# Attention in a two-layer trunk: the first map's scaling on ScalarE, norm factors inside the weight splits, four buffers for turned maps

## The chip, the cores and the metric

The kernel runs on one core of a Trainium2 chip, as one launch. The core has TensorE (PE in the profile, with its weight loads apart as PEld), VectorE (DVE), ScalarE (ACT), GpSimd (POOL), and SyncE (SP), which issues most DMAs. The metric is the device time in microseconds.

## The reference, cut to what matters

The input is 1024 positions of 1024 float32 features. Layer 0 is a diagonal state-space layer with a gated output; the change does not touch it. Layer 1 is causal differential attention with 8 heads. Each head has two score maps of 64-wide queries and keys and one 128-wide value:

```
xn = rmsnorm(h, g)                      # g: one gain per feature, for K/V and for Q/z
qz = xn @ in_w;  kv = xn @ kv_w         # q, k get a partial rotary embedding
p  = softmax(q1 k1^T / 8) - lam * softmax(q2 k2^T / 8)      # causal
o  = rmsnorm(p @ v, subln_g) * (1 - lam_init) * silu(z)
h  = h + o @ out_w                      # and a final rmsnorm
```

## The kernel before

All matrices stay close to float32 accuracy by a split: a tile is written as a rounded half, hi, and the rest, lo = x - hi, and each product is three matmuls (hi hi, hi lo, lo hi; `mm3`, L159 to L161). So every weight tile that comes from HBM is first split.

`load_m` does that for a weight tile of 128x1024: a DMA into the one buffer mraw (L739), for normed inputs a multiplication by the gain on GpSimd (L741), the cast to hi on ScalarE (L742), the subtraction to lo on VectorE (L743). `load_early` does the same once, for the keys of head 0, into tiles of the pool `pp`. Of the loads with a gain, k, q and gate have eight slices of 128 output columns with one gain per partition in each slice; the value loads (L785) have four slices of 256 columns.

Layer 1 goes through 32 steps, 4 blocks of 256 queries for each of 8 heads. In a step the scores of the next step are emitted first, then the projections of the next head by a fixed plan (nothing, keys, queries, gate and, for every second head, values), then this step's maps are transposed (`turn`) and multiplied by the values (`mix`).

`scores` handles two query blocks of 128 rows. For each, TensorE writes both maps into PSUM (L833, L834), VectorE adds the mask and takes the row extreme (L839), ScalarE takes the exponential with the row sum beside it (L841), VectorE inverts both sums in one instruction (L844), makes rho = sum1 * lam / sum2 (L845) and e1 + rho * e2 (L847), and GpSimd scales the result by 1/sum1 (L848). L is the number of keys, 128 to 1024.

`turn` transposes a map in 128x128 blocks into PSUM (L866) and splits it into ph (ScalarE, L868) and pl (VectorE, L869), one pair of tiles for two key blocks, so up to four pairs in a step. The pool `pp` has three buffers of each. `mix` multiplies them by the values (L882 to L884); `head_norm` (L899 to L907) follows with the norm and the gate.

In `project_kq` a copy of a projection, xe, is taken to SBUF (L759), and four DMAs move its rotary rows into another tile (L763), which GpSimd multiplies (L764). In `gate` a tile e holds the clamped gate (L699), which goes three times through ScalarE (L700 to L702) before VectorE uses it (L703). Both tiles have the name ze and share two buffers.

The order of instructions on each engine is not the order of the code: the framework plans it, from its own estimates of what each instruction takes, and places waits on semaphores. Each engine then works through its list in order.

Of the kernel before, what the change touches and what calls it, by code (L numbers as in the profile page):

```python
# [18 lines left out]
P = 128  # L19
# [35 lines left out]
class Trunk:  # L55
# [635 lines left out]
    def gate(self, h, zg):  # L691

        nc = self.nc
        V, G, S = nc.vector, nc.gpsimd, nc.scalar
        for hs, pt in self.project(self.I["b_in_w"], D + h * P, self.sm("gb")):
            z = self.tq.tile([P, 512], F32, name="z", tag="xr", bufs=3)
            e = self.tq.tile([P, 512], F32, name="ze", bufs=2)
            V.tensor_mul(z, pt, self.R1[:, hs])  # L698
            V.tensor_scalar(e, z, -80.0, None, op0=ALU.max)  # L699
            S.activation(e, e, AF.Exp, scale=-1.0)  # L700
            S.activation(e, e, AF.Ln, bias=1.0)
            S.activation(e, e, AF.Exp, scale=-1.0)  # L702
            V.scalar_tensor_tensor(z, z, self.small1[:, 0:1], e, op0=ALU.mult, op1=ALU.mult)  # L703
            nc.sync.dma_start(zg[:, hs], z)
# [14 lines left out]
    def load_early(self, src, col, gain):  # L719

        nc = self.nc
        raw = self.wp.tile([P, KT, P], F32, name="mraw", bufs=self.wraw)
        nc.sync.dma_start(raw, src[:, col:col + P].rearrange("(k p) n -> p k n", p=P))
        nc.gpsimd.tensor_mul(raw, raw, gain.unsqueeze(2).broadcast_to([P, KT, P]))
        w = []
        for k in range(0, KT, 4):
            hi, lo = (self.pp.tile([P, 4, P], F32R, name=n) for n in ("ph", "pl"))
            nc.scalar.copy(hi, raw[:, k:k + 4])
            nc.vector.tensor_sub(lo, raw[:, k:k + 4], rd(hi))
            w += [(hi[:, j, :], lo[:, j, :]) for j in range(4)]  # L730
        return w

    def load_m(self, src, k0, nk, col, n, gain=None, slots=None):

        nc = self.nc
        pool, names = slots or (self.wp, ("mhi", "mlo"))
        hi, lo = (pool.tile([P, nk, n], F32R, name=x) for x in names)
        raw = self.wp.tile([P, nk, n], F32, name="mraw", bufs=self.wraw)
        nc.sync.dma_start(raw, src[k0 * P:(k0 + nk) * P, col:col + n].rearrange("(k p) n -> p k n", p=P))  # L739
        if gain is not None:  # L740
            nc.gpsimd.tensor_mul(raw, raw, gain[:, k0:k0 + nk].unsqueeze(2).broadcast_to([P, nk, n]))  # L741
        nc.scalar.copy(hi, raw)  # L742
        nc.vector.tensor_sub(lo, raw, rd(hi))  # L743
        return hi, lo

    def project_kq(self, h, src, gain, kind, w=None):
# [7 lines left out]
            out = [self.st.tile([P, SEQ], F32R, name=f"k{i}") for i in range(2)]  # L754
        for i, (hs, pt) in enumerate(self.project(src, h * P, gain, early=h == 0 and kind == "q", w=w)):
            xr = self.tq.tile([P, 512], F32, name="xr", bufs=3)
            xe = self.tq.tile([P, 512], F32, name="ze", bufs=2)
            xs = self.xs[i]
            S.copy(xe, pt)  # L759
            V.tensor_mul(xr, pt, self.RC[:, hs])  # L760
# [53 lines left out]
    def scores(self, ks, qs, qb):  # L814
# [5 lines left out]
        for i in (2 * qb, 2 * qb + 1):  # L820
# [14 lines left out]
            for m in range(2):  # L835
# [5 lines left out]
                S.activation(em[:, :L], em[:, :L], AF.Exp, bias=nmx[:, m:m + 1], scale=-1.0,  # L841
                             accum_out=sm[:, m:m + 1])
                e.append(em)
            V.reciprocal(rr, sm)  # L844
            V.scalar_tensor_tensor(rho, sm[:, 0:1], self.small1[:, 1:2], rr[:, 1:2], op0=ALU.mult, op1=ALU.mult)  # L845
            p = e[0]
            V.scalar_tensor_tensor(p[:, :L], e[1][:, :L], rho, p[:, :L], op0=ALU.mult, op1=ALU.add)  # L847
            G.tensor_scalar(p[:, :L], p[:, :L], rr[:, 0:1], 1.0, op0=ALU.mult, op1=ALU.mult)  # L848
            out.append(p)
        return out  # L850

# [62 lines left out]
    def layer1(self, dbg=None):  # L914
# [5 lines left out]
        with ExitStack() as es:  # L920
# [17 lines left out]
            for z in self.padded:  # L938
                for x in z:
                    G.memset(x.bitcast(F32), 0.0)  # L940
            self.ep, self.pp, self.op, self.tiny = pool("ep", 2), pool("pp", 3), pool("op", 2), pool("tiny", 4)
            self.pst, self.pss = pool("pst", 2, space=PSUM), pool("pss", 2, space=PSUM)
            self.psm = self.rp.enter_context(tc.tile_pool(name="psm", bufs=2, space=PSUM, side="right",
                                                          reuse_waits="tile"))
# [226 lines left out]
```

## Time and profile before

| what | us |
|---|---|
| median of 3 runs | 1117.68 (1115.88 to 1118.76) |
| profiled execution, its own time | 1121.34 |
| its span | 1119.6 |
| PE busy | 1070.6 |
| DVE busy | 820.1 |
| ACT busy | 546.3 |
| POOL busy | 361.9 |

The span runs from the first to the last instruction. Matmuls overlap and their ends are modelled, so that a busy PE is not always PE at its peak; the idle time of its weight loads shows more.

### The profile page before, as it was taken

The page shows a single profiled execution, that of the slowest core. Times are in us where ns is not written, and L with a number is a line of the kernel's source. Part 1 is how long each engine was busy: PE and PEld are TensorE (multiplying, and loading weights), DVE is VectorE, ACT ScalarE, POOL GpSimd, SP SyncE. Part 2 cuts the span into 40 slices and gives each one's busy share as a digit, 9 for nine tenths or more (in the row PEclk, how much of TensorE's full clock was granted, in tenths as well). Part 3 has the DMA queues.
Part 4 walks back from the last instruction along what each step waited for, and adds up shares of the span by engine and source line. Part 5 has one row for each costly group of instructions (what it writes and reads, how often), then busy time and mean ns, then how long its engine had stood idle before and what let it go on. Part 6 is the DMA issues. An engine that isn't in the chain of part 4 may idle for free.

```text
span 1119.6 us, 17333 instructions
## 1 busy us (share of the span) xinstructions
PE 1070.6 (96%) x6308; PEld 907.6 (81%) x6308; DVE 820.1 (73%) x1362; ACT 546.3 (49%) x1141; POOL 361.9 (32%) x333
## 2 busy tenths in 40 slices
PE   7999999998999999999999999999999999999996
PEld 5688888886888888988877987889878798777796
DVE  7799999974576443557977659867597767885466
ACT  6432433234444332435755655656556466674463
POOL 0000000000564014324543345343453535421258
PEclk9999999998999999999999999999999999999998
DMA  9143555455644444123221222122221122552344
GB/s 283 37 144 124 172 171 154 141 171 199 215 132 132 150 132 169 57 57 97 65 62 44 70 65 73 52 62 72 62 75 57 57 76 79 152 167 81 94 139 158
DMA packets 143140, 125.92 MB, mean 112 GB/s; under 512 B 9808, under 2 KB 123216, under 8 KB 143056
## 3 DMA queue, kind: packets, MB, share of 16 engines
q1 hardware_dynamic: 134736, 120.63, 34.9%
q10 hardware_dynamic: 8320, 4.19, 1.2%
q8 instruction: 49, 0.80, 0.3%
q14 instruction: 35, 0.29, 0.1%
HBM read 85.48 MB, written 33.03 MB: 106 GB/s over the span
## 4 chain that ended last, share of the span: by engine, by line
PE 41%; DVE 29%; ACT 9%; DMA 9%; issue 6%; POOL 3%; SPq 2%; DVEq 0%; POOLq 0%; ACTq 0%
PE ps L159 6%; PE ps L160 6%; PE ps L161 6%; DVE w L310 5%; DMA xs<-ze 3%; DVE mlo L743 2%; PE pm L159 2%; PE pm L161 2%; ACT e L841 2%; PE pm L160 2%; PE pm L803 2%; PE pm L805 2%; PE pm L804 2%; SPq L763 2%; DVE e L839 2%
## 5 line engine op out<-in xcount | busy, mean ns | idle before, releaser
L743 DVE TENSOR_TENSOR mlo<-mraw,mhi 128x1024 fp32r<-128x1024 f32 (+1 forms) x75 | 97.8, 1304 | 61.0 <-ACT mhi L742 60.9
L159 PE MATMUL pm<-h1h,mhi 128*128 128x512 f32 x352 | 139.7, 397 | 1.7 <-DVE xr L760 1.6
L161 PE MATMUL pm<-h1h,mlo 128*128 128x512 f32 x352 | 139.6, 397 | 0.0
L160 PE MATMUL pm<-h1l,mhi 128*128 128x512 f32 x352 | 139.3, 396 | 0.0
L841 ACT ACTIVATE e<-e,tiny 128x256 f32<-128x256 f32 (+7 forms) x128 | 99.4, 777 | 80.6 <-DVE tiny L839 80.3
L742 ACT CAST mhi<-mraw 128x1024 fp32r<-128x1024 f32 (+1 forms) x75 | 77.8, 1037 | 118.4 <-PE ps L160 62.8
L839 DVE CUSTOM_DVE_ANT_0 e<-s,tri 128x256 f32<-128x256 f32 (+7 forms) x128 | 94.6, 750 | 17.1 <-PE s L834 5.9
L848 POOL TENSOR_SCALAR e<-e,tiny 128x128 f32<-128x128 f32 (+3 forms) x64 | 60.9, 952 | 119.4 <-DVE e L847 96.3
L159 PE MATMUL ps<-xh,mhi 128*128 128x512 f32 x208 | 82.2, 395 | 1.9 <-DVE evo L491 1.9
L161 PE MATMUL ps<-xh,mlo 128*128 128x512 f32 x208 | 81.9, 394 | 0.0
L160 PE MATMUL ps<-xl,mhi 128*128 128x512 f32 x208 | 81.7, 393 | 0.0
L159 PEld LDWEIGHTS pm<-h1h,mhi 128*128 128x128 f32 x352 | 66.5, 189 | 14.4 <-DVE xr L760 2.4
L161 PEld LDWEIGHTS pm<-h1h,mlo 128*128 128x128 f32 x352 | 66.6, 189 | 12.6
L160 PEld LDWEIGHTS pm<-h1l,mhi 128*128 128x128 f32 x352 | 66.5, 189 | 12.3
L833 PE MATMUL s<-k,q 128*128 128x384 f32 (+4 forms) x192 | 67.4, 354 | 7.3 <-DVE tiny L839 5.7
L803 PE MATMUL pm<-mhi,h1h 128*128 128x256 f32 x224 | 64.4, 289 | 1.7 <-DVE z L698 1.1
L834 PE MATMUL s<-k,z 128*128 128x384 f32 (+4 forms) x192 | 65.5, 345 | 0.0
L869 DVE TENSOR_TENSOR pl<-t,ph 128x512 fp32r<-128x512 f32 (+2 forms) x112 | 54.8, 494 | 14.5 <-ACT ph L868 14.1
L741 POOL TENSOR_TENSOR mraw<-mraw,small 128x1024 f32<-128x1024 f32 x23 | 45.8, 1993 | 58.1 <-DMA mraw<-in_b_in_w 35.9
L805 PE MATMUL pm<-mhi,h1l 128*128 128x256 f32 x224 | 64.1, 287 | 0.0
L804 PE MATMUL pm<-mlo,h1h 128*128 128x256 f32 x224 | 63.6, 285 | 0.2 <-DVE mlo L743 0.2
L764 POOL TENSOR_TENSOR xs<-xs,RS 128x512 f32<-128x512 f32 x32 | 44.2, 1383 | 60.5 <-DMA xs<-ze 60.3
(374 smaller groups left out, 3019.7 us busy)
## 6 DMA issues: line engine op xcount, KB each, us to landing
mraw<-in_kv_w SPq DMA_DIRECT2D x16, 512.0 KB
mraw<-in_b_in_w SPq DMA_DIRECT2D x16, 512.0 KB
mraw<-in_in_w SPq DMA_DIRECT2D x13, 512.0 KB
ud<-evo SPq DMA_DIRECT2D x16, 256.0 KB
ug<-ud SPq DMA_DIRECT2D x8, 512.0 KB
kd<-ks SPq DMA_DIRECT2D x8, 512.0 KB
toep<-kd SPq DMA_DIRECT2D x8, 512.0 KB
yd<-yb ACTq DMA_DIRECT2D x8, 512.0 KB
```

The lines of the kernel that those rows point to most:

```text
L159: mm(ps, wh, xh, start=first, stop=False)
L160: mm(ps, wh, xl, start=False, stop=False)
L161: mm(ps, wl, xh, start=False, stop=last)
L742: nc.scalar.copy(hi, raw)
L743: nc.vector.tensor_sub(lo, raw, rd(hi))
L803: mm(o, self.h1h[k][:, ts], wh, start=k == 0, stop=False)
L804: mm(o, self.h1h[k][:, ts], wl, start=False, stop=False)
L805: mm(o, self.h1l[k][:, ts], wh, start=False, stop=k == KT - 1)
L833: mm(sps[m][:, c, :w], q2[m][:, qt], ks[m][:, cs], start=True, stop=False)
L834: mm(sps[m][:, c, :w], q2[2 + m][:, qt], ks[m][:, cs], start=False, stop=True)
L839: V.tensor_tensor_reduce(out=blocks(em[:, :L]), in0=sp[:, 0:nb, :w], in1=blocks(self.tri[:, SEQ - L:]), scale=-1.0, scalar=3e38, op0=ALU.a ...
L841: S.activation(em[:, :L], em[:, :L], AF.Exp, bias=nmx[:, m:m + 1], scale=-1.0, accum_out=sm[:, m:m + 1])
```

## The change

In `scores` VectorE inverts each row sum by itself, right after its exponential; ScalarE multiplies the first map by its inverse sum in place, rho becomes lam / sum2, and the scaling on GpSimd is gone. In `load_early` and `load_m` the multiplication by the gain on GpSimd is gone; a new function `split` writes hi = raw * gain on ScalarE and lo = raw * gain - hi on VectorE, slice by slice, with the slice's gain per partition. The pool `pp` has four buffers of each tile in place of three; ze has one in place of two.

```
-            e = self.tq.tile([P, 512], F32, name="ze", bufs=2)
+            e = self.tq.tile([P, 512], F32, name="ze", bufs=1)
...
-        nc.gpsimd.tensor_mul(raw, raw, gain.unsqueeze(2).broadcast_to([P, KT, P]))
         w = []
         for k in range(0, KT, 4):
             hi, lo = (self.pp.tile([P, 4, P], F32R, name=n) for n in ("ph", "pl"))
-            nc.scalar.copy(hi, raw[:, k:k + 4])
-            nc.vector.tensor_sub(lo, raw[:, k:k + 4], rd(hi))
+            self.split(hi, lo, raw[:, k:k + 4], gain[:, k:k + 4])
             w += [(hi[:, j, :], lo[:, j, :]) for j in range(4)]
         return w
+    def split(self, hi, lo, raw, gain):
+        for k in range(raw.shape[1]):
+            g = gain[:, k:k + 1]
+            self.nc.scalar.activation(hi[:, k, :], raw[:, k, :], AF.Copy, scale=g)
+            self.nc.vector.scalar_tensor_tensor(lo[:, k, :], raw[:, k, :], g, rd(hi[:, k, :]), op0=ALU.mult,
+                                                op1=ALU.subtract)
...
         if gain is not None:
-            nc.gpsimd.tensor_mul(raw, raw, gain[:, k0:k0 + nk].unsqueeze(2).broadcast_to([P, nk, n]))
+            self.split(hi, lo, raw, gain[:, k0:k0 + nk])
+            return hi, lo
...
-            xe = self.tq.tile([P, 512], F32, name="ze", bufs=2)
+            xe = self.tq.tile([P, 512], F32, name="ze", bufs=1)
...
-            V.reciprocal(rr, sm)
-            V.scalar_tensor_tensor(rho, sm[:, 0:1], self.small1[:, 1:2], rr[:, 1:2], op0=ALU.mult, op1=ALU.mult)
+                V.reciprocal(rr[:, m:m + 1], sm[:, m:m + 1])
+                if m == 0:
+                    S.activation(em[:, :L], em[:, :L], AF.Copy, scale=rr[:, 0:1])
+            V.tensor_mul(rho, rr[:, 1:2], self.small1[:, 1:2])
             p = e[0]
             V.scalar_tensor_tensor(p[:, :L], e[1][:, :L], rho, p[:, :L], op0=ALU.mult, op1=ALU.add)
-            G.tensor_scalar(p[:, :L], p[:, :L], rr[:, 0:1], 1.0, op0=ALU.mult, op1=ALU.mult)
...
-            self.ep, self.pp, self.op, self.tiny = pool("ep", 2), pool("pp", 3), pool("op", 2), pool("tiny", 4)
+            self.ep, self.pp, self.op, self.tiny = pool("ep", 2), pool("pp", 4), pool("op", 2), pool("tiny", 4)
```

## Rows read from the trace of the kernel before

**Rows 1.** The page's head: the span.
```profile
span 1119.6 us, 17333 instructions
```

**Rows 2.** Stages: length, then busy us per engine (instructions), granted TensorE clock, DMA.
```profile
480.00:1065.00 585.00, 559.33 (x3160) 480.96 (x3159) 438.50 (x847) 339.24 (x771) 241.40 (x217) 1.00 0.27 77
640.00:660.00 20.00, 20.00 (x126) 18.16 (x126) 11.76 (x33) 10.86 (x30) 7.92 (x9) 1.00 0.23 65
680.00:700.00 20.00, 17.65 (x85) 14.10 (x86) 19.40 (x28) 11.43 (x22) 12.46 (x9) 1.00 0.27 70
```

**Rows 3.** Waits of TensorE's weight loads, 480 to 1065 us: total, times, longest.
```profile
PEld s L833 <- DVE tiny L839: 9.3, 11, 2.1
...
PEld pm L159 <- ACT oh L988: 3.4, 3, 2.0
PEld pm L159 <- ACT mhi L742: 3.0, 2, 1.6
...
PEld t L866 <- POOL e L848: 2.2, 2, 1.5
PEld t L866 <- ACT sq L901: 2.0, 3, 0.8
...
PEld t L882 <- DVE pl L869: 0.2, 1, 0.2
```

**Rows 4.** Lines on GpSimd, 480 to 1065: count, busy us, mean ns, idle before.
```profile
L848 POOL TENSOR_SCALAR e<-e,tiny 128x128 f32<-128x128 f32 (+3 forms) x64 | 60.9, 952 | 119.4 <-DVE e L847 96.3 <-DVE pl L869 8.8 <-PE s L834 5.7
...
L741 POOL TENSOR_TENSOR mraw<-mraw,small 128x1024 f32<-128x1024 f32 x21 | 42.0, 2002 | 55.3 <-DMA mraw<-in_b_in_w 35.9 <-DMA mraw<-in_kv_w 9.3 <-DVE z L703 5.6
...
L741 POOL TENSOR_TENSOR mraw<-mraw,gq 128x1024 f32<-128x1024 f32 x7 | 14.2, 2025 | 13.8 <-DMA mraw<-in_b_in_w 11.2 <-DVE tiny L845 1.4 <-DVE tiny L839 1.2
```

**Rows 5.** Timeline from 601 us: start, length, instruction.
```profile
601.74 1.90 POOL L741 TENSOR_TENSOR mraw<-mraw,small 128x1024 f32<-128x1024 f32 x1 [0.73 <-DVE xr L765]
...
601.89 2.55 DVE L847 SCALAR_TENSOR_TENSOR e<-e,tiny,e 128x768 f32<-128x768 f32 x1
```

**Rows 6.** Lines on VectorE by form, 480 to 1065 us.
```profile
L743 DVE TENSOR_TENSOR mlo<-mraw,mhi 128x1024 fp32r<-128x1024 f32 x30 | 39.2, 1308 | 15.1 <-ACT mhi L742 14.9
...
L845 DVE SCALAR_TENSOR_TENSOR tiny<-tiny,small 128x1 f32<-128x1 f32 x64 | 19.9, 311 | 1.7
...
L771 DVE TENSOR_TENSOR k<-xr,k 64x512 fp32r<-64x512 f32 x16 | 18.9, 1181 | 0.5
...
L810 DVE SCALAR_TENSOR_TENSOR vl<-pm,rcol,vh 128x128 fp32r<-128x128 f32 x48 | 16.5, 344 | 10.0 <-ACT vh L809 9.9
...
L844 DVE RECIPROCAL tiny<-tiny 128x2 f32<-128x2 f32 x64 | 10.4, 162 | 15.4 <-ACT e L841 15.0
...
L847 DVE SCALAR_TENSOR_TENSOR e<-e,tiny,e 128x768 f32<-128x768 f32 x8 | 9.7, 1208 | 0.2
```

**Rows 7.** Instructions of line 771: shortest, median, longest ns.
```profile
L771 DVE TENSOR_TENSOR k<-xr,k x16: 687/1131/2274, 488.9 to 956.3; 64x512 fp32r<-64x512 f32 x16
```

**Rows 8.** Lines on ScalarE, 480 to 1065 us.
```profile
L841 ACT ACTIVATE e<-e,tiny 128x256 f32<-128x256 f32 (+7 forms) x128 | 99.4, 777 | 80.6 <-DVE tiny L839 80.3
...
L742 ACT CAST mhi<-mraw 128x1024 fp32r<-128x1024 f32 (+1 forms) x39 | 39.9, 1023 | 41.7 <-DMA mraw<-in_b_out_w 16.4 <-POOL mraw L741 15.1 <-PE pm L161 5.2
...
L809 ACT ACTIVATE vh<-pm,rcol 128x128 fp32r<-128x128 f32 x48 | 17.6, 366 | 13.9 <-PE pm L805 8.4 <-DVE vl L810 5.5
```

**Rows 9.** Timeline at 459 us: start, length, two instructions merged in a row.
```profile
459.36 0.63 ACT L809 ACTIVATE vh<-pm,rcol 128x128 fp32r<-128x128 f32 x2 [0.98 <-POOL rcol L684]
459.76 0.61 DVE L810 SCALAR_TENSOR_TENSOR vl<-pm,rcol,vh 128x128 fp32r<-128x128 f32 x2 [0.58 <-ACT vh L809]
```

**Rows 10.** The chain that ended last, 499 to 503 us: start, length, what.
```profile
499.09 1.22 DVE mlo L743
...
502.52 1.96 DMA xs<-ze
```

**Rows 11.** Waits of ScalarE, 480 to 1065 us.
```profile
ACT ph L868 <- PE t L866: 7.6, 10, 2.2
```

## The prediction

> **What bounds the kernel now.** I read the page's busy shares first, then a table of stages, then what TensorE's weight loads wait for, and last the lines of the three other engines. All edits lie in the second layer and take effect between about 480 and 1065 us, so that stage is what counts. There TensorE is busy 559.3 of 585 us, VectorE 438.5 (75%), ScalarE 339.2 (58%) and GpSimd 241.4 (41%) [rows 2]. TensorE's work does not change (the same matmuls and transposes), so the change can only move TensorE's idle time: 585 - 559.3 = 25.7 us by that row. The weight loads, whose ends are not modelled, show a little more. Their 21 kinds of waiting sum to 42.3 us, and by releaser to 27.5 VectorE (13 kinds), 10.8 ScalarE (5), 3.3 GpSimd (2) and 0.7 issue (1); the first, the last and the ones used here stand in [rows 3]. So VectorE is the second bound. That is also where the holes are: in 680 to 700 us VectorE is busy 19.4 of 20 us and TensorE only 17.65; in 640 to 660 VectorE is at 11.8 and TensorE is full [rows 2].
>
> **GpSimd loses work.** In the stage 28 weight multiplications at L741 (42.0 + 14.2 us) and 64 scalings of the map at L848 (60.9 us) go, 117.1 of its 241.4 us [rows 4]. Its own queue was seldom late: TensorE waited 2.2 us for L848 [rows 3]. That much is a direct gain, since the transposes then follow L847 at once.
>
> What GpSimd's work does to VectorE may weigh more. L741 starts at 601.74 and runs 1.90 us; L847 starts inside it, at 601.89, and takes 2.55 us [rows 5], where the mean of its 128x768 form, the disturbed ones included, is 1208 ns [rows 6]. The shortest L771 takes 687 ns, their mean is 1181 [rows 6, 7]: 16 x 0.494 = 7.9 us lost. The same, mean less an undisturbed instruction, for L743, L845, L847, L765, L770, L771, L779, L780 and L699 together gives 43 us in the stage (four of the nine stand in [rows 6]). The removed lines are 117.1/241.4 = 49% of GpSimd's time, which gives 21 us back by share; their instructions are the longer ones, so I take 25. The bounds are 0 (other GpSimd work meets the same VectorE instructions instead) and 43.
>
> The Trainium skill ("SBUF — State Buffer", section "Who interferes with whom") says that a VectorE instruction with two SBUF inputs and a GpSimd instruction that reads SBUF exclude one another for a whole instruction. The pair in [rows 5] agrees, 2.55 us where 128x768 otherwise is near 1. By that rule the new VectorE pieces, two SBUF inputs each, can still be held up by what GpSimd keeps.
>
> **VectorE, the splits.** For the 22 loads of k, q and gate weights in the stage, one L743 of 1.22 us undisturbed (mean 1308 ns) [rows 6, 10] becomes eight 128x128 scalar_tensor_tensor. L810 is the same form from PSUM: 344 ns each, and two in 0.61 us, so 0.266 us from start to start [rows 6, 9]. Eight take 0.344 + 7 x 0.266 = 2.21 us, +0.99 a load, +21.8 in all. Each of the 6 loads of v weights becomes four 128x256, about 0.48 us and 0.40 from start to start (an estimate, between L810 at 128 and L847 at 768): 1.68, +0.46, +2.8 in all. If no piece overlapped the one before, it would be +1.53 x 22 + 0.70 x 6 = 38. The reciprocal is issued twice a block instead of once: 64 x 162 ns = +10.4 [rows 6]. L845 turns from a scalar_tensor_tensor into a product of the same size: nothing. Sum +35 (48 at the upper end) less 25 given back: +10 us, 438.5 to 448, 77%. VectorE's load hardly changes, but its longest uninterruptible pieces (1.2 us for a weight, 2.5 when stretched) give way to pieces of 0.3, and what stands behind them in the in-order queue (L839, which frees the score banks, L869, L698) waits less.
>
> **ScalarE, the splits and the map.** A load was one L742 of 1.02 us. It becomes eight 128x128 activations with a scale per partition; L809 is that form: 366 ns, two in 0.63 us, so 0.264 from start to start [rows 8, 9], 0.366 + 7 x 0.264 = 2.21 us, +1.19, x 22 = 26.2. For v weights, by the same estimate, +0.68 x 6 = 4.1. The first map's scaling is 64 activations of the shapes of L841, whose 128 have a mean of 777 ns [rows 8]: +49.7. Together +80 us (98 if nothing overlaps): 339.2 to 419, 72% of the stage. It lies beside TensorE's work as long as ScalarE keeps idle time; when that cover is gone it costs what the rival below says. Behind the scaling in ScalarE's queue stand the second exponential or the next L868; ahead of it stand the exponential, its accumulator read and VectorE's reciprocal, so ScalarE can be left waiting for VectorE once a block, 64 times.
>
> **The smaller parts.** With one ze in place of two, a writer has to wait for the last reader of the one before. For k and q these are DMAs that land 1.96 us after the last is under way [rows 10]; for the gate it is VectorE's own L703. In the order of before, 5 of 31 successive writes begin too early for one buffer, by 2.3 us in all, most of it in the one whose DMA stands in [rows 10]; so 0 to 2.3 us of ScalarE or VectorE standing still, of which I take 1 us for TensorE. If the new order put all 31 within the landing time, it would be 31 x 1.96 = 61 us of engine waiting. The fourth ph and pl: nothing in the waits names the mix matmuls (L882 to L884) as what L868 waits for, its largest releaser is the transpose in PSUM, 7.6 us [rows 11]. I cost it at nothing; it cannot give more than those 7.6 us. load_early, before 480 us, lies under a full TensorE: nothing.
>
> **The sum, in TensorE's idle time.** Of the 27.5 us for VectorE I take off a third: an equal load, but shorter pieces and fewer stretched ones (the four k and q lines hold 23 of the 43 us of stretch and stand ahead of the scores): -9. GpSimd: -2.2. Of ScalarE's 10.8 us, 6.4 are the out projection's own loads (L988, L742) [rows 3] and stay; the other 4.4 are L901, L890 and L889 holding up the transposes and the mix. ScalarE's idle share falls from 42 to 28%, which I let raise these by two thirds: +3. ze: +1. Sum -7. The profiled execution took 1121.34 us with a span of 1119.6 [rows 1]; it becomes 1114. Against the median of the runs, 1117.68, which lies 3.7 below the profiled one, the forecast is 1110.5 us, its own range 1105 to 1114.
>
> **Rivals.** *Nothing to be seen.* What VectorE gets back is spent by the +35 of the splits, and the gain of 2.2 at L848 by ze and ScalarE. For it: VectorE's load stays at three quarters either way. Against it: the stretched pieces are where they hurt. Time 1117, within 1114.3 and 1121.
>
> *ScalarE's queue becomes the bound (slower).* The place is the score step. The first map's scaling waits for VectorE's reciprocal, and in that time the in-order ScalarE does nothing. From L841's accumulator to the scaling there is at least the reciprocal's 0.16 us, and with one L847 of 1.2 us ahead of it that much more [rows 6]: 64 x 0.16 to 1.36 = 10 to 87 us more of ScalarE, 429 to 506 of 585 us. It decides from about 85% busy, the share near which VectorE shows its holes now; there ScalarE's 4.4 us of waits, and the 9.3 us in which scores wait for L839 [rows 3], would about double: +13 less the -2 of GpSimd, +11, time 1129. For it: ScalarE already waits 80.3 us for L839's result [rows 8], so it is kept in order behind VectorE. Against it: it has 246 us idle.
>
> *A larger gain.* If the mutual blocking is what makes the holes, VectorE gets back most of the 43 us and not 25. Its load then falls to about 430, and two thirds of its 27.5 us go: -18, with GpSimd -20, time 1098. For it: the stage at 680 us, where VectorE is full, has GpSimd at 12.5 of 20 us, against 7.9 at 640 [rows 2]. Against it: 124 us of GpSimd's work stay, and the 22 x 8 new pieces read two SBUF tiles each. The Trainium skill's rule on the shared port (same page and section) points at this case.
>
> *The edits don't do what they say.* The order of instructions is planned anew, by the planner's own costs, and a worse order can undo any of this. It has no price of its own; it is in the range.
>
> **Chances.** Forecast 0.40, larger gain 0.13, nothing to be seen 0.20, slower 0.27. This kernel's runs spread by 0.26%, so I count 0.3% (3.4 us: below 1114.3, above 1121.0) as what can be told from no change. Faster 0.53, the same 0.20, slower 0.27. The range goes from 1097, the larger gain, to 1127, short of the slower rival's centre.
>
> **What would show it.** After the change GpSimd should be near 240 us in all instead of 362, VectorE within 20 of its 820, and ScalarE near 620 instead of 546. L771 and L779 should have means nearer 0.85 than 1.1 us. TensorE's waits for VectorE should be under 22 us. The forecast is wrong if weight loads wait for ScalarE lines by more than 15 us in the stage, if the splits run at 0.34 us a piece with gaps between them, or if writes to ze appear among TensorE's releasers.

## The result, and the profile after

The changed kernel takes 1093.28 us (median of 4 runs, 1090.38 to 1096.06) against 1118.22 for the kernel before on the same chip (4 runs, 1115.88 to 1119.63): a ratio of 0.976, 95% interval 0.973 to 0.979. It is 25 us faster. The forecast was 1110.5, in a range from 1097 to 1127: the sign was right, the size (7 us) was under a third of the real one, and the time lies below the range. The profiled execution took 1093.5 us.

The page's head and its line of engines [rows 1]:

```profile
span 1091.7 us, 17715 instructions
...
PE 1061.9 (97%) x6308; PEld 908.2 (83%) x6308; DVE 822.5 (75%) x1617; ACT 623.9 (57%) x1396; POOL 235.3 (22%) x237
```

VectorE (820.1 before), ScalarE (546.3) and GpSimd (361.9) are where the prediction put them: within 20 of 820, near 620, near 240. The line numbers shift: the splits are now L735 (ScalarE) and L736 (VectorE), the map's scaling is L853, and L839, L841, L847 of before are L846, L848, L856.

The stages, with the columns of [rows 2]. The second layer's stage, 480 to 1065 us before, now ends at about 1040; the last row is what follows it:

```profile
480.00:1040.00 560.00, 552.72 (x3163) 483.74 (x3162) 440.87 (x1085) 414.87 (x1009) 121.66 (x124) 0.99 0.29 82
640.00:660.00 20.00, 20.00 (x115) 17.60 (x114) 15.34 (x51) 17.68 (x52) 4.73 (x7) 1.00 0.29 83
680.00:700.00 20.00, 20.00 (x103) 17.01 (x103) 18.33 (x42) 15.20 (x36) 4.66 (x4) 1.00 0.38 111
...
1040.00:1092.00 52.00, 42.01 (x346) 41.16 (x344) 33.50 (x60) 25.43 (x63) 36.97 (x47) 0.94 0.45 144
```

25 of the 28 us of span go in the stage: the same matmuls (3163 against 3160) take 560 us in place of 585. VectorE still works for 440.9 us, so its share has risen, from 75 to 79%, while TensorE is full in the stretch at 680 us in which it had lost 2.35 of 20 (the two stretches do not hold quite the same work).

What TensorE's weight loads wait for in that stage (total, times, longest) [rows 3]:

```profile
PEld s L840 <- DVE ze L699: 3.2, 1, 3.2
PEld pm L159 <- DVE xr L767: 2.4, 4, 1.1
PEld pm L810 <- DVE z L698: 1.2, 2, 0.9
PEld s L840 <- DVE tiny L846: 1.2, 5, 0.4
PEld pm L161 <- DVE mlo L750: 1.1, 1, 1.1
PEld t L874 <- ACT sqh L898: 1.0, 1, 1.0
...
PEld pm L811 <- DVE mlo L736: 0.3, 1, 0.3
```

The 13 kinds sum to 13.4 us against 42.3: 10.8 by VectorE (27.5 before), 2.6 by ScalarE (10.8), none by GpSimd (3.3). The 28.9 us that went match the 27.9 us by which the span is shorter. The scores' wait for the row extreme, 9.3 us in [rows 3], is 1.2.

The longest of these waits, 3.2 us, stands under a write of ze (L699), but the gate's ze is no input of the scores. The matmul behind that weight load waits 3.0 us for a DMA that moves half of the queries, and the chain that ended last runs through that DMA (waits of TensorE's matmuls; then the chain, start and length):

```profile
PE s L840 <- DMA q<-z: 3.0, 1, 3.0
...
950.15 4.79 DMA q<-z
```

So 7.6 us by VectorE and 3.2 by that DMA is the better reading.

Two lines of VectorE in the stage, a split and the second product of the keys, with the columns of [rows 6]:

```profile
L736 DVE SCALAR_TENSOR_TENSOR mlo<-mraw,small,mhi 128x128 fp32r<-128x128 f32 x120 | 39.3, 377 | 6.0 <-ACT mhi L735 5.8
...
L778 DVE TENSOR_TENSOR k<-xr,k 64x512 fp32r<-64x512 f32 x16 | 12.9, 806 | 0.5
```

all instructions of that product, shortest, median and longest [rows 7]:

```profile
L778 DVE TENSOR_TENSOR k<-xr,k x16: 686/687/1741, 493.1 to 937.9; 64x512 fp32r<-64x512 f32 x16
```

and two lines of ScalarE, a split and the map's scaling [rows 8]:

```profile
L735 ACT ACTIVATE mhi<-mraw,small 128x128 fp32r<-128x128 f32 (+1 forms) x144 | 48.4, 409 | 7.1 <-DMA mraw<-in_b_in_w 5.4 <-PE pm L160 1.3 <-PE pm L812 0.3
...
L853 ACT ACTIVATE e<-e,tiny 128x128 f32<-128x128 f32 (+3 forms) x64 | 48.9, 774 | 2.2 <-DVE tiny L851 1.9
```

The scaling costs 48.9 us of ScalarE (49.7 forecast), and ahead of it ScalarE waits for the reciprocal 1.9 us in all. The median L778 went from 1131 ns [rows 7] to 687. A whole load by pieces, in the timeline (start, length, pieces merged), costs VectorE 2.22 us, as forecast (2.21), and ScalarE 2.45 (2.21 forecast):

```profile
650.07 2.45 ACT L735 ACTIVATE mhi<-mraw,gq 128x128 fp32r<-128x128 f32 x8 [0.62 <-DMA mraw<-in_b_in_w]
...
650.68 2.22 DVE L736 SCALAR_TENSOR_TENSOR mlo<-mraw,gq,mhi 128x128 fp32r<-128x128 f32 x8
```

Two rows in the waits of VectorE and GpSimd before, 480 to 1065 us, which the prediction did not price (the second shows in [rows 4] only within the idle time ahead of L741):

```profile
DVE xr L765 <- POOL xs L764: 36.6, 20, 4.4
...
POOL mraw L741 <- DMA mraw<-in_b_in_w: 47.1, 12, 11.4
```

and the rows of after, on VectorE and ScalarE, that answer to them, with ScalarE's wait for the row extreme, which was 80.3 us for L839 in [rows 8]:

```profile
DVE xr L772 <- POOL xs L771: 17.5, 15, 2.3
...
ACT mhi L735 <- DMA mraw<-in_b_in_w: 9.4, 5, 3.6
...
ACT e L848 <- DVE tiny L846: 32.5, 33, 2.2
```

VectorE had stood 36.6 us for the rotary product on GpSimd, in whose queue the weight products were; now 17.5. ScalarE, with 76 us more to do in a shorter stage, waits 48 us less for the row extreme.

### The profile page after: what moved, and what is told of

It is laid out like the page before. It is cut to its first block, busy times and chain, and to the rows that moved or that the text cites. A ratio compares the mean times of both kernels' runs of the same rounds, so it can differ in the third digit from the quotient of the medians.

```text
span 1091.7 us, 17715 instructions
## 1 busy us (share of the span) xinstructions
PE 1061.9 (97%) x6308; PEld 908.2 (83%) x6308; DVE 822.5 (75%) x1617; ACT 623.9 (57%) x1396; POOL 235.3 (22%) x237
## 5 line engine op out<-in xcount | busy, mean ns | idle before, releaser
L848 ACT ACTIVATE e<-e,tiny 128x256 f32<-128x256 f32 (+7 forms) x128 | 99.3, 777 | 33.6 <-DVE tiny L846 32.5
L846 DVE CUSTOM_DVE_ANT_0 e<-s,tri 128x256 f32<-128x256 f32 (+7 forms) x128 | 94.8, 750 | 11.9 <-PE s L841 6.3
L750 DVE TENSOR_TENSOR mlo<-mraw,mhi 128x1024 fp32r<-128x1024 f32 (+1 forms) x44 | 59.9, 1360 | 42.7 <-ACT mhi L749 42.5
L749 ACT CAST mhi<-mraw 128x1024 fp32r<-128x1024 f32 (+1 forms) x44 | 45.3, 1030 | 76.0 <-PE ps L160 55.0
L159 PEld LDWEIGHTS pm<-h1h,mhi 128*128 128x128 f32 x352 | 66.2, 188 | 14.7 <-DVE xr L767 2.4
L161 PEld LDWEIGHTS pm<-h1h,mlo 128*128 128x128 f32 x352 | 66.2, 188 | 12.7
L771 POOL TENSOR_TENSOR xs<-xs,RS 128x512 f32<-128x512 f32 x32 | 42.9, 1340 | 156.0 <-DMA xs<-ze 114.2
L915 POOL TENSOR_TENSOR ob<-ob,sq 128x256 f32<-128x256 f32 x32 | 25.7, 803 | 190.3 <-ACT sq L910 177.9
L841 PE MATMUL s<-k,z 128*128 128x384 f32 (+4 forms) x192 | 65.9, 346 | 0.0
L735 ACT ACTIVATE mhi<-mraw,small 128x128 fp32r<-128x128 f32 (+1 forms) x152 | 51.8, 414 | 21.5 <-PE ps L160 14.4
L877 DVE TENSOR_TENSOR pl<-t,ph 128x512 fp32r<-128x512 f32 (+2 forms) x112 | 54.9, 492 | 10.8 <-ACT ph L876 10.4
```

The lines of the kernel that those rows point to most:

```text
L159: mm(ps, wh, xh, start=first, stop=False)
L161: mm(ps, wl, xh, start=False, stop=last)
L841: mm(sps[m][:, c, :w], q2[2 + m][:, qt], ks[m][:, cs], start=False, stop=True)
L846: V.tensor_tensor_reduce(out=blocks(em[:, :L]), in0=sp[:, 0:nb, :w], in1=blocks(self.tri[:, SEQ - L:]), scale=-1.0, scalar=3e38, op0=ALU.a ...
L877: V.tensor_sub(pl[:, jj, ii, :], tp[:, jj, ii, :], rd(ph[:, jj, ii, :]))
```

## The experiments

Each is set against the kernel before, run on the same chip. "TensorE's waits" are the sum of the view of waits of its weight loads from 480 us to 54 us before the end; the last two columns sum VectorE's waits, from 480 to 960 us, by the engine waited for. "ze n" and "pp n" are the numbers of buffers. The ballast kernels (e7, e12, e16) and the touch kernels (e17, e18) add an instruction whose result nobody reads; the others compute what the kernel before does.

| run | us (range) | ratio [95%] | TensorE's waits | VectorE for ScalarE | VectorE for GpSimd |
|---|---|---|---|---|---|
| before (pp 3, ze 2) | | 1 | 43.5 | 55.0 | 35.8 |
| after (pp 4, ze 1) | 1093.3 (1090.4 to 1096.1) | 0.976 [0.973, 0.979] | 13.4 | 59.6 | 17.5 |
| e1 map on ScalarE only | 1108.1 (1105.5 to 1112.9) | 0.989 [0.986, 0.992] | 22.7 | 51.8 | 27.3 |
| e2 pools only (pp 4, ze 1) | 1116.9 (1113.5 to 1120.7) | 0.996 [0.994, 0.998] | 34.3 | 52.1 | 33.9 |
| e3 folded gain only | 1098.5 (1095.3 to 1099.3) | 0.980 [0.977, 0.982] | 12.7 | 50.5 | 17.7 |
| e4 both edits, pp 3, ze 2 | 1099.6 (1099.3 to 1101.4) | 0.981 [0.979, 0.983] | 17.1 | 50.3 | 21.1 |
| e5 pieces, gain on GpSimd | 1118.8 (1115.6 to 1121.2) | 0.997 [0.995, 0.999] | 35.6 | 47.4 | 26.0 |
| e6 gain on ScalarE, own step | 1135.0 (1131.4 to 1136.1) | 1.011 [1.007, 1.015] | 48.8 | 90.2 | 22.2 |
| e7 after, pp 3, unread product of raw | 1153.5 (1151.4 to 1154.6) | 1.028 [1.025, 1.031] | 51.9 | 67.8 | 9.5 |
| e8 before, ze 1, two raw buffers | 1111.2 (1109.5 to 1113.0) | 0.991 [0.987, 0.994] | 23.5 | 60.4 | 27.0 |
| e9 after with pp 3, the control | 1103.5 (1101.7 to 1109.8) | 0.985 [0.981, 0.989] | 20.5 | 58.9 | 13.4 |
| e10 e9, two raw buffers | 1104.2 (1103.6 to 1105.2) | 0.984 [0.982, 0.987] | 14.8 | 51.5 | 22.2 |
| e11 e6, ze 1, two raw buffers | 1125.1 (1120.6 to 1126.1) | 1.004 [1.002, 1.006] | 30.9 | 86.1 | 21.4 |
| e12 e9, unread product of hi | 1163.5 (1163.3 to 1164.1) | 1.037 [1.034, 1.040] | 78.8 | 55.0 | 16.2 |
| e13 after without the score edit | 1103.3 (1101.7 to 1104.4) | 0.985 [0.982, 0.988] | 20.1 | 59.0 | 16.5 |
| e14 gain on VectorE, own step | 1109.9 (1108.5 to 1111.7) | 0.990 [0.987, 0.994] | 28.6 | 33.1 | 13.9 |
| e15 e6 by pieces | 1144.1 (1142.7 to 1147.9) | 1.022 [1.018, 1.025] | 55.7 | 98.3 | 19.4 |
| e16 e12, a quarter of the product | 1107.8 (1106.3 to 1109.1) | 0.989 [0.986, 0.992] | 25.6 | 58.4 | 14.6 |
| e17 e9, GpSimd touches raw | 1111.9 (1110.7 to 1113.0) | 0.994 [0.992, 0.996] | 22.2 | 59.3 | 13.0 |
| e18 e9, ScalarE touches raw | 1117.9 (1114.8 to 1121.8) | 0.999 [0.997, 1.000] | 29.7 | 68.9 | 9.9 |

The theories came up one after the other: GpSimd's instructions stretch VectorE's, that is, make them take longer than the same instruction takes elsewhere (T2a, the prediction's own "larger gain"); pieces in place of 1.2 us instructions let VectorE's queue move (T2b); a shorter chain from landing to lo frees the raw buffer sooner (T2c); and last, a first step that is ready early waits for its DMA at the head of an in-order queue, and what stands behind it is late (T5). The quoted expectations use these letters; T1 to T4 are explained in the first of them, and T2 in the first runs covers T2a and T2b.

### Which edit does it: e1 to e4, e13

e1 takes over the score edit alone (VectorE's reciprocals, ScalarE's scaling, rho):

```
+                    S.activation(em[:, :L], em[:, :L], AF.Copy, scale=rr[:, 0:1])
...
-            G.tensor_scalar(p[:, :L], p[:, :L], rr[:, 0:1], 1.0, op0=ALU.mult, op1=ALU.mult)
```

> Only the map's scaling goes to ScalarE; the gain stays on GpSimd, pools as before. If GpSimd's step at the end of the score chain (T1: L847 to L848 to the transposes) held the transposes and the weight buffers behind it, most of the 25 us come here: about 1100. If what counts is that GpSimd's long two-input instructions stretch VectorE's (T2), this removes half of GpSimd's removed time but only its one-input instructions: -6, about 1112. If the pools make the gain (T3): 1118. If only the plan's order is luckier (T4), no part need give anything like its share.

e2 takes over the numbers of buffers alone (both tiles named ze, and pp):

```
-            xe = self.tq.tile([P, 512], F32, name="ze", bufs=2)
+            xe = self.tq.tile([P, 512], F32, name="ze", bufs=1)
...
-            self.ep, self.pp, self.op, self.tiny = pool("ep", 2), pool("pp", 3), pool("op", 2), pool("tiny", 4)
+            self.ep, self.pp, self.op, self.tiny = pool("ep", 2), pool("pp", 4), pool("op", 2), pool("tiny", 4)
```

> Only four ph and pl in place of three and one ze in place of two. T3 (a fourth turned pair lets TensorE transpose ahead of the mix): about 1100, with TensorE's waits for L869 (7.8 us) gone. T1 and T2, and my prediction's own step: 1118 to 1120, nothing or slightly slower through ze.

e3 takes over the split with the folded gain alone:

```
-            nc.gpsimd.tensor_mul(raw, raw, gain[:, k0:k0 + nk].unsqueeze(2).broadcast_to([P, nk, n]))
+            self.split(hi, lo, raw, gain[:, k0:k0 + nk])
+            return hi, lo
```

> Only the gain folded into the splits, pools as before, L848 still on GpSimd. T2 (long GpSimd instructions stretch VectorE's, and 1.2 us pieces become 0.3): most of the gain, about 1102, with VectorE's mean at L771 and L779 falling from 1.1 to about 0.8 us. T1 (GpSimd's step at the end of the score chain): 1115. T3: 1118.

e4 has both edits, with the buffers of before (ze 2, pp 3).

> Both moves off GpSimd, pools as before. If the pools matter little (T1, T2): 1093 to 1097, as the whole change. If they make the gain (T3): 1110 or more. With e1 and e3 it shows whether the two moves add up: sum of their gains equal to this one's (independent), or less (either is enough), or more (only both free GpSimd).

e13 is the changed kernel with the score step of before:

```
-                V.reciprocal(rr[:, m:m + 1], sm[:, m:m + 1])
-                if m == 0:
-                    S.activation(em[:, :L], em[:, :L], AF.Copy, scale=rr[:, 0:1])
...
+            G.tensor_scalar(p[:, :L], p[:, :L], rr[:, 0:1], 1.0, op0=ALU.mult, op1=ALU.mult)
```

> The whole change without its score edit: gain folded into the splits, four ph and pl, one ze; the map is scaled by GpSimd as before. With three buffers the score edit on top of the fold gave nothing (1098.5 alone, 1099.6 with it), though alone it gave 12. If that holds with four buffers too: 1089 to 1096, as the whole change. If the score edit needs the fourth buffer: 1100 or more.

Measured: the fold alone gives 22 of the 25 us, and its interval (0.977 to 0.982) overlaps that of the whole change. The score edit alone gives 12, between the 6 of T2 and the some 18 of T1; the buffers alone give 4, so T3 falls. They do not add. With pp 3 and ze 2 the score edit adds nothing to the fold (e4 1099.6, e3 1098.5; 1093 to 1097 had been expected of T1 and T2); with pp 4 and ze 1 it is worth 10 (e13 1103.3, after 1093.3). The new numbers of buffers gain 6 us beside both edits (e4 to after) and lose 5 beside the fold alone (e3 to e13). So the fold is the main term, and what the rest gives depends on its company.

### Pieces, or the work taken off GpSimd: e5, e14

e5 keeps the product on GpSimd and makes only cast and subtraction slice by slice:

```
+        self.nc.gpsimd.tensor_mul(raw, raw, gain.unsqueeze(2).broadcast_to([P, nk, n]))
+        for k in range(nk):
+            self.nc.scalar.copy(hi[:, k, :], raw[:, k, :])
+            self.nc.vector.tensor_sub(lo[:, k, :], raw[:, k, :], rd(hi[:, k, :]))
```

> Pools, map and gain on GpSimd as before; only the cast and the subtraction of a normed weight go slice by slice (8 of 128 columns, 4 of 256) in place of one instruction each. The gain's product on GpSimd stays ahead of them. If small pieces in the in-order queues make the fold's gain (T2b): about 1102. If it is GpSimd's product itself, by stretching VectorE's instructions or as a step of the load's chain (T2a): 1118 or more, since VectorE gets 25 us more work.

e14 keeps all steps whole and puts the product on VectorE, in front of the cast:

```
-            nc.gpsimd.tensor_mul(raw, raw, gain[:, k0:k0 + nk].unsqueeze(2).broadcast_to([P, nk, n]))
+            nc.vector.tensor_mul(raw, raw, gain[:, k0:k0 + nk].unsqueeze(2).broadcast_to([P, nk, n]))
```

> The kernel before with the gain's product moved from GpSimd to VectorE, one 128x1024 instruction: GpSimd is as free as in the fold, VectorE gets some 34 us more (as much as by the fold's pieces), ScalarE nothing, and a load's chain is shorter than before by some 0.7 us. All pieces stay large. If freeing VectorE from GpSimd is what pays (T2a): 1098 to 1106. If the fold needs its small, overlapping pieces (T2b): 1115 to 1125.

Pieces alone give 2 us (0.997 [0.995, 0.999]), with 16 us more of VectorE's busy time (836.4 against 820.1), so smaller instructions by themselves are not what helps. e14 gains 11 us (1109.9, between its two expectations) although it loads VectorE, the second bound, with 31 more products at this line. 23 of them are in this row (line of VectorE, whole run):

```profile
L741 DVE TENSOR_TENSOR mraw<-mraw,small 128x1024 f32<-128x1024 f32 x23 | 28.5, 1239 | 25.6 <-DMA mraw<-in_kv_w 13.1 <-DMA mraw<-in_b_in_w 12.5
```

With 8 others of 1.22 us that is 38 us of work, 34.8 of it behind 480 us. Yet VectorE's busy time behind 480 us is 484.3 us, 10.5 more than before: some 24 us came back from other instructions, as T2a would have it. VectorE's waits for GpSimd fell as well, from 35.8 to 13.9 us. What GpSimd does to VectorE, by the one way or the other, is thus worth more than the work itself.

### The price of GpSimd's instructions: e9, e12, e16, e7

The controls and ballasts use pp 3, for the unread tile needs the room. e9 is the changed kernel with that one edit:

```
-            self.ep, self.pp, self.op, self.tiny = pool("ep", 2), pool("pp", 4), pool("op", 2), pool("tiny", 4)
+            self.ep, self.pp, self.op, self.tiny = pool("ep", 2), pool("pp", 3), pool("op", 2), pool("tiny", 4)
```

> The changed kernel with three ph and pl and one ze: the control for the next three. Between the whole change (1093) and both moves with three ph, pl and two ze (1100): 1097 to 1103; more would mean that the single ze costs something.

e12 adds to e9 a product of each finished hi tile on GpSimd, into a tile that nobody reads:

```
+        side = self.side.rearrange("p (k n) -> p k n", n=n)[:, 0:nk]
+        self.nc.gpsimd.tensor_mul(side, rd(hi), self.R1.rearrange("p (k n) -> p k n", n=n)[:, 0:nk])
```

> The control, with a GpSimd product of the size of the old L741 for each split weight, reading the finished hi tile and the norm rows and writing a tile that nobody reads. Unlike the first ballast it holds no mraw and does not run against its own split. If GpSimd's hold on VectorE is a main cause (T2a): 10 us or more over the control, VectorE's excess up by 15 us or more. If the chain and mraw are (T2c): within 4 us of the control.

e16 is the same with 256 of the 1024 columns:

```
+        nk = 256 // n
...
+        self.nc.gpsimd.tensor_mul(side, rd(hi)[:, 0:nk], self.R1.rearrange("p (k n) -> p k n", n=n)[:, 0:nk])
```

> As the ballast behind the split, but of 128x256 in place of 128x1024, some 0.6 us each. The large one added about 57 us of excess to VectorE and 60 us to the time. If the time follows VectorE's stretch about one to one (T2a): stretch up by 10 to 18 us and the time by as much, 1112 to 1121. If the large ballast did its harm otherwise (held hi tiles, GpSimd's queue): under 1108.

e7 multiplies raw in place of hi, and so also holds the raw buffer:

```
+        self.nc.gpsimd.tensor_mul(side, raw, self.R1.rearrange("p (k n) -> p k n", n=n)[:, 0:nk])
```

> The changed kernel with three ph and pl, and beside every split GpSimd does a product of the same size as the old L741, of mraw and the norm rows, into a tile that nobody reads. It stands in no chain ahead of the split; it only keeps GpSimd and the shared reads busy, and holds mraw until it is done. If stretching of VectorE makes the gain (T2a): back to 1108 to 1115, with the excess of VectorE's instructions up by some 20 us. If pieces or the shorter chain do (T2b, T2c): 1098 to 1102.

The pieces of the split on VectorE in e9:

```profile
L736 DVE SCALAR_TENSOR_TENSOR mlo<-mraw,small,mhi 128x128 fp32r<-128x128 f32 x120 | 37.9, 367 | 3.6 <-ACT mhi L735 3.4
...
L736 DVE SCALAR_TENSOR_TENSOR mlo<-mraw,gq,mhi 128x128 fp32r<-128x128 f32 x56 | 16.2, 347 | 0.3
...
L736 DVE SCALAR_TENSOR_TENSOR mlo<-mraw,small,mhi 128x256 fp32r<-128x256 f32 x24 | 11.3, 512 | 0.0
```

and in e12, with GpSimd's product, and behind them TensorE's two largest waits there:

```profile
L736 DVE SCALAR_TENSOR_TENSOR mlo<-mraw,small,mhi 128x128 fp32r<-128x128 f32 x120 | 75.1, 672 | 4.5 <-ACT mhi L735 4.5
L736 DVE SCALAR_TENSOR_TENSOR mlo<-mraw,gq,mhi 128x128 fp32r<-128x128 f32 x56 | 30.6, 600 | 8.9 <-ACT mhi L735 8.9
L736 DVE SCALAR_TENSOR_TENSOR mlo<-mraw,small,mhi 128x256 fp32r<-128x256 f32 x24 | 20.3, 895 | 0.0
...
L740 POOL TENSOR_TENSOR side<-mhi,R 128x1024 f32<-128x1024 f32 x31 | 75.9, 2447 | 104.1 <-ACT mhi L735 104.0
```

```profile
PEld s L843 <- DVE tiny L849: 20.3, 24, 3.4
PEld pm L159 <- DVE xr L770: 19.7, 12, 2.7
```

The same 200 pieces take 126.0 us in place of 65.4, 60.6 more (56 more for all of VectorE behind 480 us, 535.7 against 479.2), and the kernel takes 60 us more (1163.5 against 1103.5). VectorE's waits for the two other engines together have not grown (71.2 and 72.3 us, table), and no wait of a split on ScalarE for the product, which holds hi, stands in e12's trace. So it is the stretch itself that reaches TensorE, at about one for one: its waits grow from 20.5 to 78.8. e16's product (0.81 us each) costs 4 us, with intervals that overlap; 1112 to 1121 had been expected, but the stretch did not come either (VectorE is busy 485.7 us behind 480 us, 6.5 more than in e9). e7 costs 50, while VectorE is busy 34 us more in the whole run; it has a route that e12 shuts out, and VectorE also waits 9 us more for ScalarE.

The Trainium skill ("SBUF — State Buffer", section "Who interferes with whom") says that a VectorE instruction with two SBUF inputs and a GpSimd instruction that reads SBUF shut one another out for a whole instruction. e12 agrees: the median piece is as short as in e9 (352 and 348 ns), and the mean is made by 32 pieces of over 1 us, 25 of which end 0.15 to 0.29 us behind the end of a product, as here (timeline of e12):

```profile
586.93 2.41 POOL L740 TENSOR_TENSOR side<-mhi,R 128x1024 f32<-128x1024 f32 x1 [1.58 <-ACT mhi L735]
...
587.09 2.40 DVE L736 SCALAR_TENSOR_TENSOR mlo<-mraw,small,mhi 128x128 fp32r<-128x128 f32 x1
```

### A step of its own on ScalarE, and the raw buffer: e6, e15, e8, e10, e11

e6 frees GpSimd as the fold does, but multiplies in place on ScalarE, slice by slice, with cast and subtraction whole:

```
+        for k in range(raw.shape[1]):
+            self.nc.scalar.activation(raw[:, k, :], raw[:, k, :], AF.Copy, scale=gain[:, k:k + 1])
+        self.nc.scalar.copy(hi, raw)
+        self.nc.vector.tensor_sub(lo, raw, rd(hi))
```

> As before, but the gain is multiplied in place by ScalarE (8 instructions a load), and the cast and the subtraction stay one instruction each of 1.0 and 1.2 us. If freeing GpSimd, and with it VectorE's stretched instructions, makes the gain (T2a): 1100 to 1104, though ScalarE gets some 70 us more. If small pieces do (T2b): 1115 to 1120.

e15 does all three slice by slice:

```
+            self.nc.scalar.copy(hi[:, k, :], raw[:, k, :])
+            self.nc.vector.tensor_sub(lo[:, k, :], raw[:, k, :], rd(hi[:, k, :]))
```

> As the slow run with the gain on ScalarE, but slice by slice: scale in place, cast, subtract, so that ScalarE and VectorE overlap within a load; ScalarE has some 30 us more to do than there. If small overlapping pieces are what that run lacked (T2b): 1100 to 1110. If ScalarE's load made it slow: 1135 or more.

e8 (before, ze 1), e10 (e9) and e11 (e6, ze 1) take raw from two buffers by turns:

```
-        raw = self.wp.tile([P, nk, n], F32, name="mraw", bufs=self.wraw)
+        raw = self.raw_tile(nk, n)
...
+            self.second = pool("rawb", 1)
```

> The kernel before with two raw weight buffers in the attention stage (three ph and pl, one ze to pay for it); GpSimd does all it did. If the fold gains because a load's chain gets shorter and mraw comes free earlier (T2c): about 1105. If GpSimd's hold on VectorE or the size of the pieces is what counts: 1117 to 1121.

> The same as the control with two raw weight buffers in the attention stage. If the fold gains because mraw comes free earlier (T2c), the second buffer has nothing left to give: within 3 us of the control. If the raw buffer still holds loads back: 6 to 10 us under it, and then also under the whole change, 1088 to 1091.

> The gain multiplied in place by ScalarE, cast and subtraction in one instruction each, as in the run that was 14 us slower than before, but with two raw weight buffers. If that run was slow because the single mraw was held long and the next DMA landed late under ScalarE's in-order queue (T2c): 1105 to 1112, ScalarE's waits for those DMAs falling from 43 to under 15 us. If large pieces, or ScalarE's load, make it slow (T2b): 1128 to 1135.

e6 and e15 are slower than the kernel before, by 14 and 23 us (e6 outside both of its expectations), though GpSimd is as free as with the fold (298.5 and 293.0 us in all, against 289.9 in e3). ScalarE's load is not the reason: e15's 630.7 us is near the changed kernel's 623.9. What differs is how late ScalarE is: VectorE waits 90 and 98 us for it, against 50 in e3. Waits in e6, of ScalarE and of VectorE, 480 to 1085 us:

```profile
ACT mraw L734 <- DMA mraw<-in_b_in_w: 29.9, 15, 4.7
...
ACT mraw L734 <- DMA mraw<-in_kv_w: 12.8, 9, 4.1
...
DVE pl L875 <- ACT ph L874: 28.3, 22, 3.4
```

ScalarE stands 43 us at weights that have not landed (9.4 after), and what VectorE needs of it stands behind. That this makes e6 slow is a reading; the next section tests it.

A second raw buffer gives nothing to the control (e10 against e9). The shorter chain (T2c) had foreseen just that, so e10 does not speak against it. e8 speaks for it in part: there the second buffer, with one ze, takes 9.5 us off the kernel before (to 1111, between the 1105 expected of T2c and the 1117 or more of the others) and brings TensorE's waits from 43.5 to 23.5, although VectorE is busy as long as before (819.9 and 820.1 us), so with the stretch in place (page of e8):

```profile
PE 1064.0 (96%) x6308; PEld 906.4 (82%) x6308; DVE 819.9 (74%) x1362; ACT 548.8 (50%) x1141; POOL 361.0 (33%) x333
```

Up to some 10 us of the fold's gain may thus come by another way than less stretch, if it is not the new order of instructions. e11 is 10 us below e6 but no faster than before. The second buffer did not do there what was expected of it: ScalarE's waits for those weights went from 43 to 40 us and not under 15, and VectorE still waits 86 us for ScalarE.

### Waiting for a landing, without work: e17, e18

The control e9 with one more instruction for each load, a product of a single column of raw, as early as the weights land; on GpSimd in e17, on ScalarE in e18:

```
+        self.nc.gpsimd.tensor_mul(self.touch, raw[:, 0, 0:1], gain[:, 0:1])
```

> The changed kernel with three ph and pl (control 1103.5), and one GpSimd instruction of a single column that reads each raw weight before its split. It adds next to no work and stretches nothing, but the plan puts it where the DMA should land, so GpSimd's in-order queue stands still until it has landed, as it did 56 us for L741 in the kernel before. Theory T5, that a load's first step at the head of a queue holds up what stands behind it (xs, L771, for which VectorE waits): 8 to 15 us over the control, 1111 to 1118, with GpSimd waiting 40 us or more for DMAs. If only the stretch of VectorE's instructions counts (T2a): within 3 us of the control.

```
+        self.nc.scalar.activation(self.touch, raw[:, 0, 0:1], AF.Copy, scale=gain[:, 0:1])
```

> The same with one ScalarE instruction of a single column (0.3 us each) in place of GpSimd's. T5: ScalarE's queue then stands still for DMAs by 30 to 50 us, as in the two runs with the gain on ScalarE (43 and 52 us), and the time rises by 20 us or more over the control, to 1123 or beyond. If those runs were slow through ScalarE's work or its large pieces: 1104 to 1108.

They cost 8.5 and 14.4 us against e9. First the waits at the touch, 480 to 1065 us, in e17:

```profile
POOL touch L733 <- DMA mraw<-in_b_in_w: 73.5, 13, 13.4
...
POOL touch L733 <- DMA mraw<-in_kv_w: 32.4, 8, 8.4
```

and in e18:

```profile
ACT touch L733 <- DMA mraw<-in_b_in_w: 19.0, 13, 3.3
ACT touch L733 <- DMA mraw<-in_kv_w: 15.2, 9, 4.5
```

GpSimd stands 106 us in e17, yet VectorE waits for it no longer than in e9 (13.0 and 13.4 us), and from 480 to 960 us TensorE's waits are no longer (9.0 and 11.7 us). GpSimd's waits in all are as long as in e9 (448 and 452 us to 54 us before the end), so the standing takes the place of other waits. What e17 loses is elsewhere. At the turn of the layers TensorE falls 24 matmuls behind; the stage from 440 to 480 us in e9:

```profile
440.00:480.00 40.00, 40.00 (x285) 37.68 (x284) 20.05 (x47) 16.53 (x42) 10.73 (x10) 1.00 0.32 105
```

and in e17, where the row has 2.25 us of idle time and a lower granted clock:

```profile
440.00:480.00 40.00, 37.75 (x261) 36.02 (x260) 16.58 (x39) 13.79 (x36) 11.92 (x15) 0.91 0.28 92
```

The hole is one wait of the weight loads, for the norm factor on GpSimd (L684) at 456 us, for which e9's order has other matmuls; the stretch right behind it, full of matmuls, runs at the lower clock (0.50 of 2.4 GHz, so 1.2):

```profile
PEld ps L688 <- POOL rcol L684: 2.1, 1, 2.1
...
457.90:463.40 5.50, 5.50 (x26) 5.50 (x27) 2.68 (x6) 1.94 (x4) 2.89 (x3) 0.50 0.34 98
```

GpSimd is not held there by a touch: it starts on L684 0.1 us behind VectorE's part of it. The rest is near the end, 2.9 us of it one late cast of an output weight at 981 us. So e17's time lies within what T5 expected (8 to 15 us), but by another way, and my theory of the wait at the head of the queue falls for GpSimd. For ScalarE it holds in part: e18 has the same hole (257 matmuls), but VectorE also waits 10 us more for ScalarE (68.9 against 58.9), and TensorE's waits grow by 9. The 20 us or more that were expected did not come.

## Why the prediction was wrong

**What was right.** The stage and the resource: TensorE's work is unchanged, and its idle time in the second layer is what went. The load of each engine came out within 10 us: ScalarE 414.9 us in the stage for 419, VectorE 440.9 for 448, GpSimd 121.7 for 124. Eight pieces on VectorE took 2.22 us for 2.21; L845, costed at nothing, gave 6 us back (311 ns, now 215). What VectorE would get back was near too: the four k and q lines, 23 of the 43 us of stretch, give back 19.6 (L770, L771, L779 and L780 from means of 981, 1181, 1098 and 913 ns to 770, 806, 676 and 699).

**The step that failed** is the one from an engine's load to TensorE's waits for it, in two terms of the sum, which came to -7 where the waits fell by 28.9. "Of the 27.5 us for VectorE I take off a third ...: -9": they fell by 16.7 (by 19.9 without the wait that was the DMA's). "+3" for ScalarE: its waits fell by 8.2. Of the 22 us that the sum is short, 8 lie in the first term and 11 in the second. The working treated stretch as load and asked how full an engine would be; VectorE is no less full than before (79% of a shorter stage), ScalarE much fuller (74% for 58), and TensorE waits less for both. A stretched instruction is a delay at its own place in the order; that the stretch stood where scores and projections were waiting is my reading of the 9.3 us for L839, now 1.2. e12 gives the rate that the step should have tried: 60.6 us of stretch, 60 us of time. It was measured by adding to the changed kernel. At that rate the 25 us that VectorE was to get back would be nearly the whole gain. That the gain is made of them is argued from it, not shown: VectorE's waits for GpSimd fell too (35.8 to 17.5 us), and e12 does not tell what that is worth; and e8 has 9.5 us with VectorE busy as long as before, so that a raw buffer that is free sooner stands as a rival for part of the gain.

**ScalarE had the wrong sign.** "+3" was forecast for its larger load; TensorE's waits for it fell from 10.8 to 2.6. Of the 6.4 us that were to stay, the output projection's own loads, 0.5 is left. The load is not what makes ScalarE late; ScalarE itself was kept by VectorE (80.3 us for the row extreme, now 32.5), and by GpSimd's weight product (15.1 us in [rows 8], which is gone). e6, e15 and e18 point to what else can: a first step that waits for weights and has VectorE's work queued behind it. Only e18 has that step without the work, and it shows 10 us of VectorE's waits by it. The folded split waits less for its DMA (9.4 us).

**GpSimd** gave 3.3 us for the 2.2 forecast. Not priced at all was VectorE's wait for L764, 36.6 us, of which 19 went.

**The buffers.** I cost the fourth ph and pl at nothing, on the ground that the waits named no shortage. Between e9 and the changed kernel, which differ in it alone, lie 10 us (7.9 between the profiled executions), and most of them arise in the last 62 us. Those of the kernel before (with the columns of [rows 2]):

```profile
1057.60:1119.60 62.00, 50.53 (x394) 48.90 (x392) 36.75 (x65) 30.68 (x75) 40.30 (x50) 0.91 0.47 147
```

of e9:

```profile
1037.60:1099.60 62.00, 47.31 (x364) 45.29 (x362) 37.33 (x64) 30.42 (x73) 39.50 (x49) 0.91 0.47 147
```

and of the changed kernel:

```profile
1029.70:1091.70 62.00, 52.31 (x413) 50.57 (x411) 37.59 (x64) 30.97 (x73) 38.93 (x49) 0.95 0.48 149
```

TensorE starts 49 matmuls more there than in e9 (at 62/413 us each, 7.4 us), is idle 9.7 us in place of 14.7, and has a higher granted clock; e13, also with four buffers, starts 412. The buffer alone does not make the number: e2 with four starts 399, and the kernels with three start from 342 (e18) to 399 (e8). One ze was costed at 1 us, by 0 to 2.3 us of an engine standing still: ScalarE waits 8.0 us for the DMAs that read it, but no wait of TensorE can be put down to it (the one under L699, which would have been one of the signs against the forecast, was the DMA of queries). e9 is 4 us above e4, which has two, with intervals that overlap.

**The rivals.** "A larger gain", at 1098, came nearest, and its reason, the mutual blocking, is the one that e12 supports; but it asked for VectorE's load to fall, and the load stayed, and it had nothing for ScalarE's 8 us, so that its nearness is partly luck. "ScalarE's queue becomes the bound" did not come: the wait for the reciprocal is 2 us. A late ScalarE goes with lost time all the same, in e6, e15 and e18, where it waits for a landing and not for VectorE.

**What stays open.** Each kernel's order is planned anew, and the order changes far from the edit (the turn of the layers in e17 and e18, the last 62 us with three buffers), so that a difference of 5 us or so between two variants can be the plan's. This may be why the score edit is worth 12, 0 or 10 us by its company; the edit and the order were not separated. How the gain divides between less stretch, a GpSimd that is sooner ready for VectorE, and a raw buffer that is free sooner is open. So are the part of e8's gain that is the buffer itself (it has no control with one ze and three pairs) and the full size of e6 and e15. None of the kernels run beats the changed kernel; e3 comes nearest, with intervals that overlap. Four buffers together with two ze were not tried.

## What to carry to other kernels

Price what a second engine does to the one that feeds TensorE as delay and not as load: where instructions stretch, count the stretch of the stage at about one for one as a first estimate (60 us for 60.6 in e12), even if the engine's busy share won't move. Fold a scale into a step that exists: as a step of its own the same product cost 11 us more on VectorE (e14 against e3) and 36 to 46 more on ScalarE (e6, e15 against e3). Before costing a buffer at nothing, look at the part of the run where little other work is left to fill TensorE, here the last 62 us. And where the view of waits names a releaser that is no input of what waits, look at the next instruction's wait: here it was a DMA.

## What the runs showed of the hardware that was not expected

- A GpSimd product of 128x1024 (2.45 us) holds, as a rule, one VectorE piece of 0.35 us to the product's end, up to 2.6 us (e12), while the median piece stays at 0.35; one of 128x256 (0.81 us) does so little that the mean goes from 367 to 393 ns: e16's time is 4 us above the control's, e12's 60.
- GpSimd can stand 106 us for DMAs in the second layer's stage without VectorE waiting longer for it (e17). Where ScalarE stands 34 us for them without other work, VectorE waits 10 us more for it (e18).
- Behind a hole of 2 us in TensorE at 456 us the granted clock is 0.50 for 5.5 us in which TensorE is busy throughout, and 0.98 in the 2.6 us after (e17); without the hole it is 1.00 over the whole stretch (e9).
